# Hybrid SSD/Conformer layer: start addresses of the streamed SBUF tiles moved to 128 modulo 256 bytes, and a selection copy moved from VectorE to ScalarE

## The chip, the cores and the metric

The kernel runs on one core of a Trainium2 chip. The metric is the device time of one execution in microseconds (us). Each core has TensorE (PE, matrix products; its weight loads are listed as PEld), VectorE (DVE), ScalarE (ACT), GpSimd (POOL) and SyncE (SP, which issues the DMAs here). SBUF is the working memory, 128 partitions wide; PSUM takes the results of matmuls. A byte address below is an offset within a partition.

## The reference

One trunk layer of a diffusion backbone over 512 latent and 128 context tokens, width 1024, in float32. Cut to what matters:

```python
h = rms_norm(x, g_mix_pre) * (1 + sc1) + sh1
z, xbc, dt_raw, cf_in = split(h @ w_in)              # 1024 -> 4640 columns
xs, B, C = split(silu(dwconv1d(xbc, 3 taps)))
y = ssd_scan(xs, dt, B, C, forward) + flip(ssd_scan(flipped)) + xs * d_skip
y_ssd = rms_norm(y * silu(z))
u = silu(layer_norm(dwconv1d(cf_a * sigmoid(cf_g), 31 taps)))
x = x + g1 * rms_norm(concat([y_ssd, u]) @ w_out)
h = rms_norm(x, g_ffn_pre) * (1 + sc2) + sh2
up = dwconv(h @ w_ffn_up)                            # 1024 -> 5632, 3x3 on the latent grid
x = x + g2 * rms_norm((silu(gate) * val) @ w_ffn_down)   # 2816 -> 1024
```

The shifts, scales and gates come from `silu(c) @ w_ada`. The SSD scan works in chunks of 128 tokens and needs, for each pair of heads and each direction, the exponential of a cumulative decay.

## The kernel before, in words

All activations stand channels by tokens: a tile is 128 channels by T = 640 tokens (512 latent, then 128 context), 2560 bytes in a partition. The large products are made from two halves in the format fp32r: a weight unit of 128x1024 is fetched (`wr`), copied to a high part `wh` by ScalarE (L165), and the rest `wl` is made by GpSimd (L167). The activations are split in the same way. `mm3` (L268) then issues, for one block of 128 input channels, three products (wh with the high activation, wh with the low one, wl with the high one), and each for the columns 0 to 384 and 384 to 640: six matmuls, 384 and 256 columns in turn. The activation tile is what TensorE streams; the weights are loaded.

The stages in order of time: modulation vectors and first projections; the input projection with 36 weight units (L268, streamed tiles H0 to H15), into which the SSD of eight head pairs (`ssd`, L590 to L674) and eight 31-tap convolutions (`conv31_sum`, L721, on DVE) are woven; the output projection in two halves of the columns (streamed tiles S and H); the FFN up projection (streamed tiles T0 to T15) with its 3x3 convolution on DVE (L1090); the down projection (streamed tiles S, T and H in turn, 22 blocks for each of 8 output blocks).

Instructions are put in order by the tile framework, which places each by a simulated timeline and priorities; each engine then runs its own in that order, and waits on semaphores. The order is fixed when the program is built.

**Addresses.** The tiles of the pool `sb` are laid one after another in order of the first use of their tag, each rounded up to 32 bytes. A later tile of the same tag gets the same place. In the program before:

| tiles | start in bytes | modulo 256 |
|---|---|---|
| T0 to T15, S0 to S3 (2560 bytes each) | 17,536 to 81,280 | 128 |
| U0, U1, M3 | 64,928, 67,680, 70,432 | 160, 96, 32 |
| `asc` (64 bytes) | 83,840 | 128 |
| S4 to S17, M0 to M7 without M3, H0 to H15, HL, AT, ysq | 83,904 to 186,304 | 192 |
| `gs2` (64 bytes) | 188,864 | 192 |
| `wr`, `wh`, `wl` (4096 bytes each) | 188,928 on | 0 |

So the tile `asc` of 8 x 2 floats is what sets every tile after it 64 bytes further on.

**The selection rows.** In `decays` (inside `ssd`), `sel` picks two heads of each direction out of an identity (`ids`), each repeated 64 times: 128x256. It is copied by `ve.tensor_copy` (L608) and then loaded as the stationary operand of two matmuls of 512 columns (L612) that spread the decays; ScalarE takes the exponential (L616). `sel` has one buffer, so the copy for pair p+1 stands after the matmuls for pair p.

Of the kernel before, what the change touches and what calls it, by code (L numbers as in the profile page):

```python
# [7 lines left out]
F32 = mybir.dt.float32  # L8
F32R = mybir.dt.float32r
AF = mybir.ActivationFunctionType  # L10
# [3 lines left out]
P = 128  # L14
# [7 lines left out]
KD = D // P  # L22
# [25 lines left out]
def hybrid_layer_kernel(ctx: ExitStack, tc: tile.TileContext, xT, ct, prm, cst, wrest, wdt, idhl_d, wada1, wada2, win,  # L48
                        wout, wup, wdown, st0, yT, nsf, nsb):
    nc = tc.nc  # L50
    te, ve, ac, gp, sy = nc.tensor, nc.vector, nc.scalar, nc.gpsimd, nc.sync

    sb = ctx.enter_context(tc.tile_pool(name="sb", bufs=1))
# [6 lines left out]
    def nm(s):  # L60
        uid[0] += 1
        return f"{s}_{uid[0]}"

    def slot(tag, dt=F32, shape=(P, T)):
        return sb.tile(list(shape), dt, tag=tag, name=nm(tag))

    def psum(i):
        return ps.tile([P, 1024], F32, tag=f"P{i}", name=nm(f"ps{i}"))

    def psq(i):  # L70
        return ps.tile([P, 512], F32, tag=f"Q{i}", name=nm(f"pq{i}"))
# [32 lines left out]
    ids = sb.tile([P, 32], F32, tag="idhl", name="ids")  # L104
# [255 lines left out]
        te.matmul(pt[32 * j:32 * j + 32, 0:c1 - c0], wdts[:, k, :], xs_[k][:, c0:c1],  # L360
                  start=k < 4, stop=k >= 4, tile_position=(0, 32 * j))

    asc = sb.tile([P, KD, 2], F32, tag="asc", name="asc")
    h_hi, h_lo = [], []
    firsts = [(get_unit(unit_of[n][0]), psum((0, 2, 1)[i])) for i, n in enumerate(FIRST)]
    for s in range(1, 4):
# [184 lines left out]
    def ssd_tokens(p):  # L551

        xs = xsp[p]
        xt = xtp[p] = slot(("S14", "T13", "S14", "T13", "S14", "M2", "S14", "M2")[p])
        to_tokens(xs, xt)
        xw = []
        for d in range(2):
            o = slot(f"S{4 + d}")
            gp.tensor_tensor(hq(o), hq(xt), WD[:, :, 16 * d + 2 * p:16 * d + 2 * p + 2].unsqueeze(3)
                             .to_broadcast([P, NCH, 2, 64]), MUL)  # L560
            xw.append(o)
        xwp[p] = xw

    def ssd_states(p):
        g = p // 4
        xw = xwp[p]

        cs = []
        for d, o in enumerate((nsf, nsb)):
            pt = psq(d)  # L570
            for s in range(3):
                c = s if d == 0 else 3 - s
                te.matmul(pt[:, s * P:(s + 1) * P], btok[g][:, c * P:(c + 1) * P],  # L573
                          xw[d][:, c * P:(c + 1) * P], start=True, stop=True)
            te.matmul(pt[:, 3 * P:4 * P], xw[d][:, 4 * P:5 * P], btok[g][:, 4 * P:5 * P], start=True, stop=True)
            t = slot(f"S{12 + d}" if p % 2 else ("S16", "AT")[d])
            ac.activation(t[:, 0:4 * P], pt, AF.Copy)  # L577
            sy.dma_start(o[p], t[:, 3 * P:4 * P])
            cs.append(t)
        prev = [[stt[p][:, d, :]] for d in range(2)]  # L580
        for s in range(3):
            for d in range(2):
                tmp = sm.tile([P, P], F32, tag="adar", name=nm("stmp"), bufs=1)
                now = cs[d][:, s * P:(s + 1) * P]
                gp.tensor_tensor(tmp.rearrange("p (h q) -> p h q", h=2),
                                 prev[d][s].rearrange("p (h q) -> p h q", h=2),
                                 CDs[:, s, d, 2 * p:2 * p + 2].unsqueeze(2).to_broadcast([P, 2, 64]), MUL)
                gp.tensor_tensor(now, now, tmp, ADD)  # L588
                prev[d].append(now)
        prevs[p] = prev  # L590

    def ssd(p):
        g = p // 4
        xs, xt, prev = xsp[p], xtp[p], prevs[p]
        last = p == NPAIR - 1
        xd = []
        for d in range(2):
            o = slot(("M4", "H11")[d] if last else f"S{2 + d}")
            a = 16 * d + 2 * p
            gp.tensor_tensor(hq(o), hq(xt), DT[:, :, a:a + 2].unsqueeze(3).to_broadcast([P, NCH, 2, 64]), MUL)  # L600
            xd.append(o)

        ea = []

        def decays():
            peas = []
            sel = sm.tile([P, 2, 2, 64], F32R, tag="sel", name=nm("sel"), bufs=1)
            ve.tensor_copy(sel, ids.rearrange("p (d h) -> p d h", d=2)[:, :, 2 * p:2 * p + 2]  # L608
                           .unsqueeze(3).to_broadcast([P, 2, 2, 64]))
            for d in range(2):  # L610
                pea = psq(d)
                te.matmul(pea[:, 0:L], sel[:, d].rearrange("p h q -> p (h q)"), acHL[:, 0:L], start=True, stop=True)  # L612
                ea.append(slot(f"S{10 + d}"))
                peas.append(pea)
            for o, pea in zip(ea, peas):
                ac.activation(o[:, 0:L], pea[:, 0:L], AF.Exp)  # L616

        if last:
            decays()

        rs = {}
        for h in range(2):
            for d in range(2):
                row = 2 * p + h + 16 * d
                sel1 = idr[:, row:row + 1].to_broadcast([P, P])
                r = slot(f"{'H' if last else 'S'}{(12 if last else 6) + 2 * h + d}")
                if last:
                    pbl = psum(2 * d)
                for q, (c0, c1) in enumerate(((0, 3), (3, 5))):
                    pb = pbl[:, 512 * q:512 * q + 512] if last else psq(q)  # L630
                    te.matmul(pb[:, 0:(c1 - c0) * P], sel1, acHL[:, c0 * P:c1 * P], start=True, stop=True)  # L631
                    for c in range(c0, c1):
                        if last and d:
                            ve.tensor_scalar(r[:, c * P:(c + 1) * P], pb[:, (c - c0) * P:(c - c0 + 1) * P],
                                             ACM[:, c, row:row + 1], 0.0, SUB, MIN)
                            continue
                        ac.activation(r[:, c * P:(c + 1) * P], pb[:, (c - c0) * P:(c - c0 + 1) * P], AF.Relu,  # L637
                                      scale=-1.0, bias=ACM[:, c, row:row + 1])
                rs[h, d] = r
        if p + 1 < NPAIR:  # L640
            ssd_tokens(p + 1)
        if not last:
            decays()
        for (h, d), r in rs.items():
            ssd_exp[0] = ac.activation(r, r, AF.Exp, scale=1.0 if last and d else -1.0)  # L645
        for i, (h, d) in enumerate(rs):
            r = rs[h, d]
            (ve if i % 2 or last else gp).tensor_tensor(r, r, cbm[g][d], MUL)  # L648
        if p + 1 < NPAIR:
            ssd_states(p + 1)  # L650

        for d in range(2):
            po = psq(d)
            for c in range(4):
                te.matmul(po[:, c * P:(c + 1) * P], prev[d][c if d == 0 else 3 - c],  # L655
                          cT[g][:, c * P:(c + 1) * P], start=True, stop=True)
            ve.tensor_tensor(ea[d][:, 0:L], ea[d][:, 0:L], po[:, 0:L], MUL)
        (ve if p > 5 else gp).tensor_tensor(ea[0][:, 0:L], ea[0][:, 0:L], ea[1][:, 0:L], ADD)

        t = slot(f"T{p}")  # L660
        for q, cc in enumerate(((0, 1, 2, 3), (4,))):
            py = psq(q)
            for i, c in enumerate(cc):
                for d in range(2):
                    for h in range(2):
                        te.matmul(py[64 * h:64 * h + 64, i * P:(i + 1) * P],  # L666
                                  xd[d][:, c * P + 64 * h:c * P + 64 * h + 64],
                                  rs[h, d][:, c * P:(c + 1) * P], start=d == 0, stop=d == 1,
                                  tile_position=(0, 64 * h))
            c0, c1 = cc[0] * P, (cc[-1] + 1) * P  # L670
            ve.scalar_tensor_tensor(t[:, c0:c1], xs[:, c0:c1], prm_col("d_skip", p), py[:, 0:c1 - c0], MUL, ADD)
        yoff[p] = ea[0]
        tp[p] = t
# [105 lines left out]
    for it in seq:  # L779
        if it[0] == "proj":  # L780
# [4 lines left out]
            elif n[0] == "a":  # L785
                p = int(n[1:])
# [10 lines left out]
            elif n[:2] == "xs":  # L797
                p = int(n[2:])
# [12 lines left out]
        elif it[0] == "ssd":  # L811
            p = it[1]
# [158 lines left out]
        y_part(m, None, BOTH, out_ps[m], False, True)  # L971
        out_done(m, BOTH, out_ps[m])
    def gains():
        gg = gains_of['post'] = sb.tile([P, KD, 2], F32, tag="asc", name="gg1")
        ve.tensor_tensor(gg, modv[:, 16:24, :], prm_col("g_mix_post", 0, 8).unsqueeze(2).to_broadcast([P, 8, 2]), MUL)
        gs = gains_of['pre'] = sb.tile([P, KD, 2], F32, tag="gs2", name="gs2")
        ve.tensor_scalar(gs, modv[:, 32:40, :], 1.0, None, ADD)
        ve.tensor_tensor(gs, gs, prm_col("g_ffn_pre", 0, 8).unsqueeze(2).to_broadcast([P, 8, 2]), MUL)

    gains_of = {}  # L980
# [266 lines left out]
    with tc.issue_after(prior[0].ins):  # L1247
        for q in range(EARLY, NF):
            split_f(q)
    gg2 = sb.tile([P, KD, 2], F32, tag="asc", name="gg2")  # L1250
    ve.tensor_tensor(gg2, modv[:, 40:48, :], prm_col("g_ffn_post", 0, 8).unsqueeze(2).to_broadcast([P, 8, 2]), MUL)
    msq = sb.tile([P, T], F32, tag="ysq", name="m2sq")
    mtags = ["H5", "H6", "S8", "S9", "S16", "S17", "U0", "U1"]
# [208 lines left out]
```

## Time and profile before

| | |
|---|---|
| median of 3 runs | 1010.86 us (1010.83 to 1013.97) |
| profiled execution | 1010.71 us, of which the span of its instructions is 1008.9 us |
| mean granted TensorE clock | 0.993 |
| busy: PE, DVE, POOL, ACT | 968.3, 736.1, 588.8, 457.9 us |

Views used below: the page of the profile; busy time by stretches of time (windows); groups of instructions by line and shape; the chain of work that ended last; and the timeline, which merges neighbours of one kind into a row (start, length, kind, count). A matmul is given about 0.28 to 0.34 us in these rows, though the next one starts 0.11 to 0.18 us after it: they overlap, and what a matmul costs is read from the starts.

### The profile page before, as it was taken

How to read it: one execution, taken by the hardware profiler on the slowest of the kernel's cores; microseconds unless marked ns; L12 is line 12 of the kernel's file. 1: busy time of each engine (PE TensorE's matmuls, PEld its weight loads, DVE VectorE, ACT ScalarE, POOL GpSimd, SP SyncE). 2: the span in 40 equal slices, each digit the busy share in tenths (PEclk: the TensorE clock that was granted, in tenths of full speed). 3: DMA queues.
4: the chain of work that ended last, by engine and by line, in shares of the span. 5: the costliest groups of instructions: out<-in, count | busy, mean ns of one | idle time of the engine just before them, and what ended most of it. 6: DMA issues, size and time to landing. Idle time of an engine off the chain costs nothing.

```text
span 1008.9 us, 18834 instructions
## 1 busy us (share of the span) xinstructions
PE 968.3 (96%) x7655; PEld 933.7 (93%) x7655; DVE 736.1 (73%) x1093; ACT 457.9 (45%) x766; POOL 588.8 (58%) x426
## 2 busy tenths in 40 slices
PE   4999999999999989999989999999999999999995
PEld 2789999999999978899979999999999999999995
DVE  3789999989999998672286798998988988400004
ACT  6244556674553856842364754233233236322211
POOL 2333877888887896443473696454454456543444
PEclk9999999999999999999999999999999999999998
DMA  9622121122212111559463422222222222222212
GB/s 345 229 80 79 53 94 63 54 74 64 74 43 66 41 50 41 167 165 391 156 206 106 147 84 64 85 70 77 85 71 76 84 70 68 79 79 74 79 37 105
DMA packets 42934, 102.76 MB, mean 102 GB/s; under 512 B 4832, under 2 KB 12768, under 8 KB 42848
## 3 DMA queue, kind: packets, MB, share of 16 engines
q1 hardware_dynamic: 42848, 101.56, 30.4%
q8 instruction: 60, 0.98, 0.4%
q14 instruction: 26, 0.21, 0.1%
HBM read 97.87 MB, written 3.67 MB: 101 GB/s over the span
## 4 chain that ended last, share of the span: by engine, by line
PE 81%; DVE 7%; ACT 5%; POOL 3%; issue 2%; DMA 2%; SPq 0%; POOLq 0%; ACTq 0%; DVEq 0%
PE ps L268 67%; PE ps L1112 3%; PE pq L268 2%; POOL wl L167 2%; PE pq L313 2%; PE pq L666 1%; DVE T L760 1%; ACT wh L165 1%; DVE ps L721 1%; PE pq L655 1%; PE pq L573 1%; DMA wr<-in_wout 1%; PE pq L294 1%; PE pq L631 1%; DMA T<-in_xT 1%
## 5 line engine op out<-in xcount | busy, mean ns | idle before, releaser
L167 POOL TENSOR_TENSOR wl<-wr,wh 128x1024 fp32r<-128x1024 f32 (+3 forms) x127 | 291.7, 2297 | 293.3 <-ACT wh L165 287.4
L268 PE MATMUL ps<-H,wh 128*128 128x384 f32 (+1 forms) x1636 | 322.1, 310 | 4.9 <-DVE M L421 2.2
L165 ACT ACTIVATE wh<-wr 128x1024 fp32r<-128x1024 f32 (+3 forms) x131 | 131.7, 1006 | 342.6 <-PE ps L268 196.8
L268 PE MATMUL ps<-T,wh 128*128 128x384 f32 (+1 forms) x1472 | 273.1, 306 | 1.9 <-ACT S L1080 1.9
L268 PEld LDWEIGHTS ps<-H,wh 128*128 128x128 f32 x1636 | 249.0, 188 | 9.1 <-issue 4.5
L1090 DVE SCALAR_TENSOR_TENSOR S<-ps,prms,S 128x441 f32<-128x441 f32 (+2 forms) x336 | 233.4, 695 | 29.7 <-ACT S L1080 19.2
L268 PEld LDWEIGHTS ps<-T,wh 128*128 128x128 f32 x1472 | 219.3, 188 | 2.3 <-ACT S L1080 2.2
L721 DVE SCALAR_TENSOR_TENSOR ps<-u,prms,ps 128x655 f32<-128x655 f32 x223 | 200.7, 900 | 9.9 <-ACT ps L718 5.4
L268 PE MATMUL ps<-H,wl 128*128 128x384 f32 (+1 forms) x818 | 194.8, 310 | 0.0
L268 PE MATMUL ps<-T,wl 128*128 128x384 f32 (+1 forms) x736 | 166.7, 306 | 0.0
L268 PEld LDWEIGHTS ps<-H,wl 128*128 128x128 f32 x818 | 128.8, 188 | 1.6 <-issue 1.2
L268 PEld LDWEIGHTS ps<-T,wl 128*128 128x128 f32 x736 | 113.0, 188 | 0.0
L341 DVE RECIPROCAL rsm<-rsm 128x160 f32<-128x160 f32 (+2 forms) x9 | 7.3, 815 | 141.5 <-ACT rsm L340 141.5
L268 PE MATMUL ps<-S,wh 128*128 128x384 f32 (+1 forms) x420 | 87.5, 312 | 1.7 <-DVE M L923 1.2
L268 PEld LDWEIGHTS ps<-S,wh 128*128 128x128 f32 x420 | 65.9, 188 | 4.3 <-issue 2.5
L268 PE MATMUL ps<-S,wl 128*128 128x384 f32 (+1 forms) x210 | 54.4, 308 | 0.3 <-POOL wl L167 0.3
L637 ACT ACTIVATE S<-pq,ACM 128x128 f32<-128x128 f32 x140 | 40.9, 372 | 18.3 <-PE pq L631 18.1
L1080 ACT ACTIVATE S<-ps,prms 128x640 f32<-128x640 f32 x42 | 36.5, 868 | 0.0
L268 PEld LDWEIGHTS ps<-S,wl 128*128 128x128 f32 x210 | 35.0, 188 | 0.5 <-POOL wl L167 0.5
L588 POOL TENSOR_TENSOR S<-S,stmp 128x128 f32<-128x128 f32 x36 | 18.6, 517 | 15.1 <-ACT S L577 11.2
L1193 POOL TENSOR_TENSOR H<-S,S 128x640 f32<-128x640 f32 x16 | 25.2, 1578 | 0.0
L648 POOL TENSOR_TENSOR S<-S,M 128x640 f32<-128x640 f32 x14 | 22.1, 1577 | 4.4 <-ACT S L645 4.4
(353 smaller groups left out, 1276.7 us busy)
## 6 DMA issues: line engine op xcount, KB each, us to landing
wr<-in_wup SPq DMA_DIRECT2D x44, 512.0 KB, 3.4
wr<-in_win SPq DMA_DIRECT2D x36, 512.0 KB, 3.5
T<-in_wada SPq DMA_DIRECT2D x49, 256.0 KB, 5.4
wr<-in_wdown SPq DMA_DIRECT2D x16, 512.0 KB, 3.4
wr<-in_wout SPq DMA_DIRECT2D x13, 512.0 KB, 3.4
H<-in_wada SPq DMA_DIRECT2D x23, 256.0 KB, 5.5
S<-in_wada SPq DMA_DIRECT2D x16, 256.0 KB, 5.9
wr<-in_wdown SPq DMA_DIRECT2D x8, 384.0 KB, 3.1
```

The lines of the kernel that those rows point to most:

```text
L165: ac.activation(hi[:, :n], raw[:, :n], AF.Copy)
L167: lo_eng.tensor_tensor(lo[:, :n], raw[:, :n], hi[:, :n].bitcast(F32), SUB)
L268: last_mm[0] = te.matmul(out, w, x[:, c0:c1], start=first and i == 0, stop=last and i == 2)
L313: te.matmul(pt[32 * j:32 * j + 32, 0:P], cts[:, kc, :], w[:, j * P:(j + 1) * P], start=kc == 0, stop=kc == KD - 1, tile_position=(0, 32 * j))
L588: gp.tensor_tensor(now, now, tmp, ADD)
L637: ac.activation(r[:, c * P:(c + 1) * P], pb[:, (c - c0) * P:(c - c0 + 1) * P], AF.Relu, scale=-1.0, bias=ACM[:, c, row:row + 1])
L648: (ve if i % 2 or last else gp).tensor_tensor(r, r, cbm[g][d], MUL)
L721: ve.scalar_tensor_tensor(acc, u[:, j:j + UO], w(j), acc, MUL, ADD)
L1080: ac.activation(out, v, AF.Identity, bias=prm_col("ffn_b", i), scale=w(1, 1))
L1090: ve.scalar_tensor_tensor(ob, vl[:, r0 + a - 1:r1 + a - 1, q0 + b - 1:q1 + b - 1], w(a, b), ob, MUL, ADD)
L1112: te.matmul(pt[:, o:o + c1 - c0], w[k] if i in (1, 2) else w[:, k * P:(k + 1) * P], x[:, c0:c1], start=k == 0 and j == 0, stop=k == KD - 1 ...
L1193: gp.tensor_tensor(f_raw[q], a, b, MUL)
```

## The change

Two parts. First, `asc`, `gg1` and `gg2` (tag `asc`) become the first 16 columns of tiles that are 64 floats wide (256 bytes), and `gs2` of one that is 32 floats wide (128 bytes). All tiles of the pool that stand after `asc` move up by 192 bytes, those after `gs2` by 256. By the same rule of placing, S4 to S17, the M and H tiles, HL, AT and ysq then start at 128 modulo 256, as T0 to T15 and S0 to S3 did already; `wr`, `wh` and `wl` stay at 0. U0, U1 and M3 stay where they were. Nothing that is computed changes. Second, the copy of `sel` is an activation with Copy on ScalarE.

```diff
-    asc = sb.tile([P, KD, 2], F32, tag="asc", name="asc")
+
+    def small(tag, name, width):
+        return sb.tile([P, width], F32, tag=tag, name=name)[:, 0:2 * KD].rearrange("p (k c) -> p k c", k=KD)
+
+    asc = small("asc", "asc", 64)
...
-            ve.tensor_copy(sel, ids.rearrange("p (d h) -> p d h", d=2)[:, :, 2 * p:2 * p + 2]
-                           .unsqueeze(3).to_broadcast([P, 2, 2, 64]))
+            ac.activation(sel, ids.rearrange("p (d h) -> p d h", d=2)[:, :, 2 * p:2 * p + 2]
+                          .unsqueeze(3).to_broadcast([P, 2, 2, 64]), AF.Copy)
...
-        gg = gains_of['post'] = sb.tile([P, KD, 2], F32, tag="asc", name="gg1")
+        gg = gains_of['post'] = small("asc", "gg1", 64)
...
-        gs = gains_of['pre'] = sb.tile([P, KD, 2], F32, tag="gs2", name="gs2")
+        gs = gains_of['pre'] = small("gs2", "gs2", 32)
...
-    gg2 = sb.tile([P, KD, 2], F32, tag="asc", name="gg2")
+    gg2 = small("asc", "gg2", 64)
```

## The prediction

> **What bounds the kernel now.** I read the page first, then busy time by stretches, then the chain that ended last.
>
> ```profile
> PE 81%; DVE 7%; ACT 5%; POOL 3%; issue 2%; DMA 2%; SPq 0%; POOLq 0%; ACTq 0%; DVEq 0%
> ```
> ```profile
> core 0: us, PE busy (x) PEld busy (x) DVE busy (x) ACT busy (x) POOL busy (x), PEclk, DMA share, GB/s
> 58.00:430.00 372.00, 360.80 (x2750) 348.57 (x2749) 342.64 (x443) 218.97 (x418) 272.80 (x230) 1.00 0.22 70
> 570.00:835.00 265.00, 264.91 (x1897) 264.54 (x1898) 239.80 (x392) 97.27 (x121) 146.06 (x80) 1.00 0.25 80
> 835.00:990.00 155.00, 155.00 (x1070) 154.72 (x1070) 30.93 (x36) 47.89 (x69) 71.60 (x35) 1.00 0.22 65
> ```
>
> Four fifths of the chain is TensorE. In the up projection (570 to 835) and the down projection (835 to 990) PE never rests, at the full granted clock; there the time is the number of matmuls times the distance of their starts. In the input projection PE works 360.8 of 372 us and DVE 342.6: PE leads, and DVE is close behind. So the distance of the starts is the first thing that a new address could change. The timeline of PE shows it: each row with `wl` closes one set of six matmuls (three pairs of 384 and 256 columns), so from one `wl` row to the next is the price of a set.
>
> ```profile
> 72.61 0.47 PE L268 MATMUL ps<-H,wl 128*128 128x384 f32 x2
> ...
> 77.11 0.47 PE L268 MATMUL ps<-H,wl 128*128 128x384 f32 x2
> ```
> ```profile
> 891.62 0.45 PE L268 MATMUL ps<-H,wl 128*128 128x384 f32 x2
> ...
> 892.48 0.45 PE L268 MATMUL ps<-H,wl 128*128 128x384 f32 x2
> ```
>
> There are two rhythms: 0.90 us a set (five sets in 4.50) and 0.86, the same shapes at the same clock. The slow one costs 0.04 us more, 13.3 ns for each pair of 384 and 256 columns. H stands at 192, and has both: slow at 73 in the input projection, fast at 891 in the down projection. A whole stage shows in the mean length of a matmul of 384 columns, about 10 ns more in the slow rhythm:
>
> ```profile
> L268 PE MATMUL ps<-H,wh 128*128 128x384 f32 x620 | 197.8, 339 | 4.9 <-DVE M L421 2.2 <-ACT T L858 1.5 <-ACT u L700 1.2
> ```
> ```profile
> L268 PE MATMUL ps<-T,wh 128*128 128x384 f32 x608 | 188.0, 332 | 1.9 <-ACT S L1080 1.9
> ```
> ```profile
> L268 PE MATMUL ps<-T,wh 128*128 128x384 f32 x112 | 34.9, 341 | 0.0
> L268 PE MATMUL ps<-H,wh 128*128 128x384 f32 x92 | 28.1, 333 | 0.0
> ```
>
> These are the groups of 58 to 430 (H, mixed), 570 to 834 (T, all but eight pairs fast) and 858 to 985 (T slow, H fast). So tiles at 128 have both rhythms too, and in the down projection, where PE streams T and H in turn, the two alternate. Counted by the starts, 242 of the 867 whole pairs of the input projection are slow and 521 fast (the others are broken by a wait or change over); between 858 and 985, 174 pairs at 128 are all slow and 229 at 192 all fast.
>
> The rhythm is not a property of the address alone. It holds while PE runs on, and is drawn again when another instruction comes between. In the up projection (the timeline of PE, then the chain):
>
> ```profile
> 621.90 0.46 PE L268 MATMUL ps<-T,wl 128*128 128x384 f32 x2
> ...
> 622.80 0.46 PE L268 MATMUL ps<-T,wl 128*128 128x384 f32 x2
> 623.10 0.64 PE L268 MATMUL ps<-T,wh 128*128 128x384 f32 x3
> 623.58 0.27 PE L276 MATMUL pq<-csts,adar 128*128 128x128 f32 x1
> ```
> ```profile
> 623.85 210.27 PE ps L268 x1467
> ```
>
> The T tiles go at 0.90 us a set before one transpose of the modulation vectors, and after it at 210.27 / 1467 = 143.3 ns a matmul, 0.86 us a set, for 210 us. Where the address changes while PE runs on, as in the down projection, the rhythm turns over with it.
>
> **The change part by part.**
>
> *Copy of sel.* Eight casts leave DVE, eight copies come to ACT.
>
> ```profile
> L608 DVE CAST sel<-ids x8: 484/1648/1829, 21.6 to 395.1; 128x256 fp32r<-128x256 f32 x8
> ...
> who waited for it (us, times):
> ```
> ```profile
> 353.30 1.56 DVE sel L608
> ...
> 357.76 0.60 DVE S L657
> ...
> 358.40 1.63 PE pq L666 x25
> ```
> ```profile
> 395.05 0.40 DVE sel L608
> ```
> ```profile
> L616 ACT ACTIVATE S<-pq 128x512 f32<-128x512 f32 x16 | 8.7, 596 | 1.9 <-PE pq L612 1.8
> ```
>
> Nobody waits for `sel`. What counts is the DVE time that it takes from others. Up to about 340 PE sets the pace and a freed DVE only waits longer: nothing, and if PE had slack there it would be worth up to the rest of the casts. In the chain the cast stands twice: 1.56 us at 353, with four DVE instructions behind it and the matmuls L666 of pair 6 waiting for the last, and 0.40 us at 395. Sum: -1.96, taken as -2.0. On ACT the nearest row has twice the columns and 0.60 us, which bounds a copy from above. ACT is busy 219 of 372 us and the copy can stand anywhere in the tens of us between two uses of `sel`, so I put it at nothing; the copy has to wait for the matmuls L612 of the pair before, and behind it in ACT's queue stand the exponentials L616 and the splits of the weights, for which GpSimd and then PE wait: if two copies stand in front of these in the chain, that is 1.2 us. Bounds: -9.9 (the six casts between 130 and 375, at the median of 1.65 us, if DVE alone set this stage) to +1.2. I take -2.0, since the chain names it.
>
> *Down projection.* All streamed tiles get one address, so the rhythm should no longer turn over between tiles. All fast: 174 x 13.3 ns = -2.3 us. All slow: 229 x 13.3 = +3.05. I take fast, since the stage is entered from the up projection in the fast rhythm at 128, though single matmuls of two products are woven around 836 and 850 and can upset it.
>
> *Input projection.* 867 pairs go from 192 to 128. Both addresses have a fast and a slow rhythm of the same price, so I take the same share: 0. All fast would be -3.2 (242 pairs), all slow +6.9 (521).
>
> *Up projection.* Its tiles stand at 128 before and after, and so do the weights at 0. The rhythm is drawn at 570 and again at 620 and 624, after products of H tiles that do move. I take fast as now: 0. If slow after 624, 731 pairs x 13.3 = +9.7; if slow from 570, 897 pairs, +11.9.
>
> *Matmuls of 256 columns alone* (second half of the output projection, last half block of the down projection). Tiles at 192 go through at 0.34 us for three, tiles at 128 at 0.355:
>
> ```profile
> 994.17 0.28 PE L268 MATMUL ps<-H,wl 128*128 128x256 f32 x1
> ...
> 995.19 0.28 PE L268 MATMUL ps<-S,wl 128*128 128x256 f32 x1
> ```
> ```profile
> 562.09 0.28 PE L1112 MATMUL pq<-T,wl 128*128 128x256 f32 x1
> ...
> 563.15 0.28 PE L1112 MATMUL pq<-T,wl 128*128 128x256 f32 x1
> ```
>
> Three sets take 1.02 and 1.06 us, so 5 ns for each matmul. About 200 are concerned, half of them mixed with tiles at 128 already: +0.5 us (0 to 1.0).
>
> *The other engines on the moved tiles.* The same ACT copy takes as long from T to H as from H to T:
>
> ```profile
> L253 ACT ACTIVATE T<-H 128x640 fp32r<-128x640 f32 x8 | 5.9, 735 | 1.9 <-PE ps L268 1.4
> L253 ACT ACTIVATE H<-T 128x640 fp32r<-128x640 f32 x8 | 5.8, 738 | 10.7 <-DVE T L385 10.6
> ```
>
> 735 against 738 ns at crossed addresses: 0, and I carry that over to DVE, POOL and DMA, hidden by PE in the two FFN stages (DVE busy 239.8 of 265 us in the first).
>
> Sum against the profiled execution: 1010.7 - 2.0 - 2.3 + 0 + 0 + 0.5 = 1006.9 us, taken as 1007.0. That execution is 0.15 us under the median of the runs, and 1.8 us of it lie outside its span.
>
> [...]
>
> **The rivals.**
>
> *A, the forecast:* 1007.0; by the uncertainty of the input projection and of sel some 1002 to 1011. Chance 0.46.
>
> *B, the down projection locks in the slow rhythm.* For it: the T tiles at 128 are slow there now, after entering fast. Against: they turned where tiles of the other address came between. 1010.7 - 2.0 + 3.05 + 0.5 = 1012.3. Chance 0.22.
>
> *C, slower: the up projection locks in the slow rhythm after 624.* One mechanism: the draw after the last transpose falls the other way and nothing interrupts 731 pairs. For it: the eight slow pairs before 623.6 are on the same tiles. Against: 897 of 912 pairs are fast now. With the down projection as in A: 1006.9 + 9.7 = 1016.6. From some 290 slow pairs on it eats the 3.8 us that A gains, from some 520 on the kernel is measurably slower. Chance 0.19.
>
> *D, the address does nothing, and both rhythms stay where they are:* only sel counts, 1008.7. Chance 0.13.
>
> **How the numbers follow.** A measurement of this kernel can tell about 0.3% from no change: 3.0 us, so faster is below 1007.8 and slower above 1013.9. Of A about two thirds lie below 1007.8, of D a third, of B a tenth: 0.31 + 0.04 + 0.02, with a little for an input projection that goes all fast: 0.39. Of C nearly all is slower, and of B and A a part (an input projection that gets slower, an order of instructions that the move of sel has shifted): 0.27. The rest, 0.34, is no measurable change. Range: downwards all of the input projection fast (-3.2) and a sel gain of 5 us give 1006.9 - 3.2 - 3.0 = 1000.7; upwards C, 1016.6. The likeliest case alone has 1002 to 1011.
>
> **What would show it.** Right: between 858 and 985 the groups of T, H and S matmuls have one mean length, 331 to 333 ns; L268 on T stays at 332 between 570 and 834; the chain around 353 and 395 has no sel; L608 is an ACT row of 0.4 to 0.6 us. Wrong: a mean of 341 in the down or up projection (B, C); the same alternation as now at one address (D); a shorter stretch from 330 to 375 than sel's own 1.6 us explains (DVE bound more than I take it to). It would be wrong above all if the rhythm follows something that I do not see in these rows, since it is worth more than all else here.

## The result, and the profile after

The changed kernel is slower: 1018.93 us median (1017.07 to 1021.56) against 1010.91 for the kernel before beside it, ratio 1.0071 with the 95% interval 1.0051 to 1.0091. The profiled execution took 1019.31 us, with a span of 1017.5 us, 8.6 more than before. The forecast was 1007.0, and its range ended at 1016.6.

The page's shares of the chain and the busy time by stretches, of the changed kernel:

```profile
PE 84%; DVE 7%; ACT 3%; POOL 2%; issue 2%; DMA 1%; SPq 0%; POOLq 0%; ACTq 0%; DVEq 0%
```
```profile
core 0: us, PE busy (x) PEld busy (x) DVE busy (x) ACT busy (x) POOL busy (x), PEclk, DMA share, GB/s
58.00:430.00 372.00, 358.14 (x2716) 346.36 (x2714) 330.50 (x434) 217.39 (x420) 271.86 (x229) 0.99 0.21 66
570.00:835.00 265.00, 263.24 (x1881) 262.65 (x1880) 235.53 (x385) 101.88 (x129) 149.33 (x83) 1.00 0.26 83
835.00:990.00 155.00, 155.00 (x1076) 155.00 (x1075) 41.60 (x53) 48.64 (x69) 75.61 (x37) 1.00 0.24 72
```

VectorE has 12 us less to do between 58 and 430 (330.50 against 342.64), about what the moved copies should give, and yet TensorE got less done there (2716 instructions against 2750). The granted clock of that stretch is 0.99 in place of 1.00. That hundredth turns out to matter.

The same places of the chain that ended last, before and then after (start, length, what):

```profile
71.94 12.41 PE ps L268 x81
85.07 8.81 PE ps L268 x59
...
291.22 3.31 PE ps L268 x21
...
374.15 3.31 PE ps L268 x21
...
570.09 48.40 PE ps L268 x336
...
623.85 210.27 PE ps L268 x1467
...
874.47 114.40 PE ps L268 x771
```
```profile
73.23 13.90 PE ps L268 x81
87.85 8.81 PE ps L268 x59
...
295.12 3.43 PE ps L268 x21
...
379.46 3.44 PE ps L268 x21
...
579.06 50.63 PE ps L268 x336
...
634.93 210.27 PE ps L268 x1467
...
884.79 112.43 PE ps L268 x771
```

Read down the starts: the changed kernel is 1.3 us late at 72, 2.8 at 85, 3.9 at 291, 5.3 at 374, 9.0 at 570, 11.1 at 624, and 10.3 at 874. So it loses 9 us up to the end of the output projection, a stretch for which the forecast had a gain of 2.0 from `sel` and little else, then 2.2 us in the first 336 products of the up projection (50.63 against 48.40), nothing in the next 1467, and wins 2.0 back in the 771 of the down projection.

Two of these rows were forecast. The down projection has one rhythm now (groups of 869 to 1000, last figure before the bar is the mean in ns):

```profile
L268 PE MATMUL ps<-T,wh 128*128 128x384 f32 x112 | 33.8, 332 | 0.0
L268 PE MATMUL ps<-H,wh 128*128 128x384 f32 x98 | 29.5, 332 | 0.0
...
L268 PE MATMUL ps<-S,wh 128*128 128x384 f32 x90 | 27.1, 332 | 0.0
```

and the copy of `sel` is a row of ScalarE, 0.42 us long (L612 in the new numbering):

```profile
L612 ACT ACTIVATE sel<-ids 128x256 fp32r<-128x256 f32 x8 | 3.3, 418 | 0.0
```

One thing was in no rival. The row of 81 products at 73 us takes 1.49 us longer than before with the same work. The windows show why: first three stretches of 3.41 us, then the stretches that follow them, all of the changed kernel.

```profile
69.95:73.36 3.41, 1.16 (x9) 0.94 (x8) 3.41 (x9) 0.20 (x1) 0.00 (x0) 1.00 0.20 80
360.08:363.49 3.41, 1.22 (x22) 1.22 (x24) 3.41 (x5) 1.15 (x3) 2.89 (x6) 1.00 0.45 135
534.16:537.57 3.41, 1.49 (x15) 1.12 (x14) 3.41 (x4) 1.56 (x5) 1.98 (x1) 1.00 1.03 366
```
```profile
73.30:76.80 3.50, 3.50 (x14) 3.50 (x15) 2.90 (x6) 3.49 (x4) 0.58 (x1) 0.51 0.00 0
363.40:366.90 3.50, 3.50 (x27) 2.51 (x24) 3.50 (x5) 0.00 (x0) 2.90 (x4) 0.51 0.00 0
537.50:541.00 3.50, 3.50 (x13) 3.50 (x12) 2.59 (x6) 2.17 (x4) 1.11 (x1) 0.51 0.64 248
```

PE was busy for 1.16 to 1.49 us of 3.41 in each of the first three, and in the stretch behind each the granted clock is half (0.51). In the profiled execution of the kernel before, the granted clock is 1.00 all the time between 30 and 1002 us. An estimate from these figures (half the clock for 3.41 us): each such stretch costs up to 1.7 us where TensorE has work throughout; the row at 73 us lost 1.49.

### The profile page after: what moved, and what is told of

Same layout as the page of the kernel before. It is cut to its first block, busy times and chain, and to the rows that moved or that the text cites. A ratio compares the mean times of both kernels' runs of the same rounds, so it can differ in the third digit from the quotient of the medians.

```text
span 1017.5 us, 18830 instructions
## 1 busy us (share of the span) xinstructions
PE 973.1 (96%) x7655; PEld 939.2 (92%) x7655; DVE 722.4 (71%) x1085; ACT 460.0 (45%) x774; POOL 589.9 (58%) x426
## 4 chain that ended last, share of the span: by engine, by line
PE 84%; DVE 7%; ACT 3%; POOL 2%; issue 2%; DMA 1%; SPq 0%; POOLq 0%; ACTq 0%; DVEq 0%
PE ps L268 69%; PE ps L1116 3%; PE pq L670 2%; PE pq L268 2%; PE pq L313 2%; DVE ps L725 1%; DVE T L764 1%; PE pq L659 1%; POOL wl L167 1%; ACT wh L165 1%; PE pq L294 1%; PE pq L577 1%; DMA T<-in_xT 1%; PE pq L635 1%; PE pq L334 1%
## 5 line engine op out<-in xcount | busy, mean ns | idle before, releaser
L268 PE MATMUL ps<-H,wh 128*128 128x384 f32 (+1 forms) x1636 | 324.4, 311 | 6.2 <-DVE M L425 2.2
L268 PE MATMUL ps<-T,wh 128*128 128x384 f32 (+1 forms) x1472 | 273.3, 306 | 1.8 <-ACT S L1084 1.8
L268 PEld LDWEIGHTS ps<-H,wh 128*128 128x128 f32 x1636 | 250.9, 189 | 11.9 <-issue 5.9
L268 PEld LDWEIGHTS ps<-T,wh 128*128 128x128 f32 x1472 | 219.4, 188 | 2.1 <-ACT S L1084 2.1
L268 PE MATMUL ps<-H,wl 128*128 128x384 f32 (+1 forms) x818 | 193.8, 310 | 0.0
L268 PE MATMUL ps<-T,wl 128*128 128x384 f32 (+1 forms) x736 | 166.8, 306 | 0.0
L268 PEld LDWEIGHTS ps<-H,wl 128*128 128x128 f32 x818 | 128.9, 189 | 0.7 <-issue 0.5
L268 PEld LDWEIGHTS ps<-T,wl 128*128 128x128 f32 x736 | 112.9, 188 | 0.0
L268 PE MATMUL ps<-S,wh 128*128 128x384 f32 (+1 forms) x420 | 87.4, 311 | 1.8 <-DVE M L927 0.9
L268 PEld LDWEIGHTS ps<-S,wh 128*128 128x128 f32 x420 | 65.9, 188 | 4.0 <-issue 2.3
L268 PE MATMUL ps<-S,wl 128*128 128x384 f32 (+1 forms) x210 | 54.3, 308 | 0.3 <-POOL wl L167 0.3
L268 PEld LDWEIGHTS ps<-S,wl 128*128 128x128 f32 x210 | 35.0, 188 | 0.5 <-POOL wl L167 0.5
```

Source lines behind the costliest of these rows:

```text
L268: last_mm[0] = te.matmul(out, w, x[:, c0:c1], start=first and i == 0, stop=last and i == 2)
```

## The experiments

The shown differences left three suspects: the addresses, the moved copy, and the half-clock stretches. Ratios are against the kernel before, run beside each kernel on the same chip, with 95% intervals; medians from different chips are not compared, since the kernel before itself moved between 1010.9 and 1014.3.

**One part at a time.** Addresses only:

```diff
+    small = lambda tag, name, w: sb.tile([P, w], F32, tag=tag, name=name)[:, 0:2 * KD].rearrange("p (k c) -> p k c", k=KD)
+    asc = small("asc", "asc", 64)
...
+        gs = gains_of['pre'] = small("gs2", "gs2", 32)
```

> Only the addresses are changed (streamed tiles at 128 modulo 256, wr/wh/wl at 0); the copy of sel stays on VectorE, and with it the order of the instructions is that of before. Theory R (the address sets the rhythm of the matmul pairs, and the loss of the changed kernel is the slow rhythm drawn in the up projection's first part, +2.2, and in the output projection, +0.6, against -2.7 in the down projection): the down projection 858 to 985 all at 331 to 333 ns, -2.3 to -2.7 us against before; in all 1008 to 1011. Theory O (the 8 us are lost by the other order that the moved copy brings): 1008 to 1010, down projection as under R, stretches before 430 within 1 us of before. Theory G (the three windows of half clock at 73, 363 and 537 us make the loss, up to 1.7 us each): if the addresses bring them, the mean granted clock falls from 0.993 to 0.984 to 0.987 here, and the time is 1014 to 1018; if not, the clock stays at 0.993.

Measured: 1012.49 us, ratio 0.9995 (0.9979 to 1.0011). The moved copy only:

```diff
-            ve.tensor_copy(sel, ids.rearrange(...)...)
+            ac.activation(sel, ids.rearrange(...)..., AF.Copy)
```

> Only the copy of sel is moved to ScalarE; all addresses are those of before. Its order of instructions is that of the changed kernel. Theory R: the down projection alternates as before (T 341, H 333 ns), the sel gain of up to 2 us stands alone: 1009 to 1011. Theory O: this kernel has the whole loss before 560, +6 to +8 us there, and the down projection's 2.3 us besides: 1017 to 1020. Theory G: the clock falls to 0.984 to 0.987 only if the other order makes the idle stretches in which the gate closes; then windows of 3.4 us at half clock near 73, 363 or 537 are in its records, and each costs about 1.7 us.

Measured: 1022.08 us, ratio 1.0092 (1.0074 to 1.0111). And both parts again:

> The changed kernel again, with both parts, on the same chip as the three others. All theories: 1017 to 1020, mean granted clock 0.983 to 0.987, windows of 3.4 us at half clock between 70 and 540 us; R: up projection slow from its start to 623 again (a draw that comes out the same in each execution) ; if the rhythm is drawn at random in each execution, it comes out otherwise here and the time moves by 2 us.

Measured: 1019.03 us, ratio 1.0071 (1.0049 to 1.0093). The moved copy carries the whole loss, and the addresses none of it. In this execution of the same program the first 166 pairs of the up projection ran in the fast rhythm, where the first profile had them slow: the rhythm of that stretch is drawn in each execution (its 336 products took 50.03 us all the same, since a half-clock stretch fell into them: the granted clock from 570 to 625 us is 0.97).

The sel-only kernel also shows what the lost time looks like. The timeline of PE, before, and then sel-only, at the last L631 of pair 7 and the 40 products L666 behind it (idle time and its releaser in brackets):

```profile
396.37 0.39 PE L631 MATMUL ps<-HL,idr 128*128 128x256 f32 x1
...
397.83 2.40 PE L666 MATMUL pq<-S,S 128*64 128x128 f32 x40
```
```profile
403.35 0.39 PE L631 MATMUL ps<-HL,idr 128*128 128x256 f32 x1 [2.08 <-DVE H L634]
...
404.25 4.07 PE L666 MATMUL pq<-S,S 128*64 128x128 f32 x40
```

L631 waits 2.08 us for VectorE, where before it did not wait: behind the last L575 in front of it the old order has 13 products of L268, the new order 8. Then the clock halves (0.50 from 404.45 to 407.86 us), and the 40 products take 4.07 us in place of 2.40.

**Is it the work or the order?** The planned order changes with the moved copy. Put in order of start, by line, shape and tiles, and without the copies themselves, the profiles of before and sel-only have another instruction at 558 of TensorE's 7655 places, at 33 of VectorE's 1085 and at 62 of ScalarE's 766. With the addresses alone it is none on any engine. Two kernels have the same work on each engine (both make the copy, one result is not read) in the two orders; f1 differs from before at 4 places of TensorE's list, f2 from sel-only at 59, all before 100 us:

```diff
 f1, order of before: sel is cast on VectorE and used
+            idle = sm.tile([P, 2, 2, 64], mybir.dt.bfloat16, tag="idle", name=f"idle{p}", bufs=1)
+            ac.activation(idle, ids.rearrange(...)..., AF.Copy)
 f2, order of sel-only: sel is copied on ScalarE and used
+            ve.tensor_copy(idle, ids.rearrange(...)...)
```

> Addresses of before; sel is cast on VectorE as before and used, and ScalarE makes the same copy besides, into a tile that nobody reads. The order on VectorE, GpSimd and SP is that of before, and TensorE's but for two places; ScalarE has eight copies more. Theory O (the order makes the loss): ratio 0.999 to 1.001, clock 0.990 to 0.993. Theory A (ScalarE's copies themselves make it, since they stand in front of other ScalarE work): ratio 1.005 to 1.009, eight rows of 0.42 us and later exponentials behind them.

> Addresses of before; sel is copied on ScalarE and used, and VectorE makes the cast besides, into a tile that nobody reads. The order on TensorE, GpSimd and SP is that of sel-only but for a few places on TensorE. The same work for each engine as in the kernel with the extra ScalarE copy, in the other order. Theory O: ratio 1.007 to 1.011, as sel-only's 1.0092 or a little more, clock 0.985 to 0.987. Theory A: the same ratio as the kernel with the extra ScalarE copy, within 0.002.

Measured: f1 1015.79 us, ratio 1.0007 (0.9989 to 1.0024); f2 1022.39 us, ratio 1.0076 (1.0052 to 1.0099). Eight copies more on ScalarE cost nothing, and giving VectorE its casts back wins nothing. The order makes the loss. (One thing besides the order differs, which of the two copies the matmuls read; the profiles of f1 and f2 list nobody as waiting for it.) f2 has the idle time of sel-only in the same place, and f1 has no idle time of that size between 390 and 410 us. In f2 no half-clock stretch followed in that execution, and the 40 products took their 2.40 us:

```profile
404.83 0.38 PE L634 MATMUL ps<-HL,idr 128*128 128x256 f32 x1 [2.11 <-DVE H L637]
...
405.73 2.40 PE L669 MATMUL pq<-S,S 128*64 128x128 f32 x40
```

**Where in the order.** Four kernels move some of the eight copies: `if p == 6`, `if p != 6`, `if 0 < p < 6`, `if p == 0`.

> Addresses of before; only the copy of sel for pair 6 (the one that stood in the chain at 353 us) is on ScalarE, the seven others on VectorE. Theory O1 (the loss of sel-only, 1.0092 of before, is one place: with this copy moved, the 25 to 40 products L666 of pair 6 and the L268 products around them change places, so that PE has nothing left to fill the wait for VectorE near 396 to 401): this kernel has the new idle time of about 2 us near 397 to 401 and is 3 to 6 us slower than before (ratio 1.003 to 1.006). Theory O2 (the loss is spread over the whole order, each moved copy brings a bit): ratio within 1.002. Theory S (my forecast's sel term: 1.6 us of VectorE in the chain saved at 353): ratio 0.998 to 0.999.

Measured: ratio 1.0015 (0.9999 to 1.0031). The idle time at L631 is there (2.53 us), and the profiled execution lost 3 us between 366 and 515 us, but over its runs the kernel is hardly slower. O1 was wrong: this is one place of several.

> Addresses of before; seven copies of sel on ScalarE, that for pair 6 on VectorE. Theory O1: no new idle time near 400, ratio 1.000 to 1.004, mean clock as before (0.990 to 0.993). Theory O2: ratio 1.006 to 1.008, clock 0.986 to 0.988. If the half-clock windows come with the first stretch (the wait at 70 us) alone: clock 0.989 to 0.991, ratio 1.002 to 1.004.

Measured: 1020.36 us, ratio 1.0061 (1.0045 to 1.0078), no idle time at L631, mean clock 0.9855. O2 was nearer.

> Addresses of before; the copies of sel for pairs 1 to 5 are on ScalarE, those for 0, 6 and 7 on VectorE. The order before 130 us and after 340 us is then nearly that of before. Theory O3 (the loss of all-but-sel6, 1.0061, comes from five copies in the middle: more idle time near 265 to 295, and a half-clock window there in some executions): ratio 1.002 to 1.005, clock 0.988 to 0.990, shift at 300 us of +1 to +2. Theory O4 (the copies in the middle are hidden by TensorE, which leads there; the loss sits at the start and at the end of the stage): ratio 0.999 to 1.001, clock as before, shift at 300 us within 0.5.

Measured: 1016.55 us, ratio 1.0043 (1.0027 to 1.0059), clock 0.983 to 0.987 in its runs. TensorE's order differs from that of before at 113 places, 97 of them L268 and L631, and yet a second wait stands right behind the one that the kernel before has at 267 us (first row before, the other two this kernel):

```profile
267.27 0.91 PE L573 MATMUL pq<-S,M 128*128 128x128 f32 x6 [1.57 <-ACT S L616]
```
```profile
264.67 0.91 PE L573 MATMUL pq<-S,M 128*128 128x128 f32 x6 [1.57 <-ACT S L620]
...
266.76 1.44 PE L268 MATMUL ps<-H,wh 128*128 128x384 f32 x4 [0.95 <-DVE S L752]
```

Together they leave PE busy for 0.43 of the stretch of 3.41 us that ends at 266, and from 266 us on this execution ran 3.41 us at half clock.

> Addresses of before; only the first copy of sel (pair 0, near 20 us) is on ScalarE. What changes in the order is the start alone: the L360 and L294 products among each other before 60 us. Theory O4: the first unit's products start 0.5 to 1.3 us later (the L165 copy at 54 us in before, 55.1 to 55.3 in three executions with the order of the changed kernel), ratio 1.0005 to 1.002. Theory O3: ratio 0.999 to 1.0005.

Measured: 1014.55 us, ratio 1.0026 (1.0010 to 1.0042), more than either theory had. Its profiled execution had the first part of the up projection slow, which is 2.2 us by chance. The parts 0.0015, 0.0043 and 0.0026 add to 0.0084 of sel-only's 0.0092 (pair 7 was not tried alone, and each part has an interval of 0.0016 to either side): the loss is spread over the whole order.

**How much of it is the clock.** In every execution profiled the half-clock stretches stand on one grid of 3.413 us (in the changed kernel they start at 73.36, 363.49 and 537.57 us, 85 and 51 times 3.413 apart); its phase to the program differs from one execution to the next (1.68 us past a whole multiple of 3.413 there, 2.42 in the profile of before, where the clock changes at 29.73 and 1002.53). Between 50 and 985 us the 18 profiles hold 39 of them, and 34 follow a grid stretch in which PE was busy for 0.28 to 0.48 of the time. All 24 stretches with at most 0.40 were followed by one, and 10 of the 18 above that and below 0.50. Five more follow stretches between 0.50 and 0.64, where most stretches are not followed (0.60 and 0.63 in the profile of before were not); what decides there I can't explain. The idle time at 70 us (2.1 to 2.3 us) is in every kernel; in the profile of before the grid cut it in two, and no half-clock stretch followed either part (compare 1.16 us busy above):

```profile
67.28:70.69 3.41, 2.41 (x18) 2.16 (x16) 3.41 (x8) 0.00 (x0) 0.00 (x0) 1.00 0.43 154
70.69:74.10 3.41, 2.16 (x14) 2.19 (x15) 3.41 (x8) 2.22 (x3) 0.00 (x0) 1.00 0.00 0
```

So the number of half-clock stretches is a draw, and the order sets its odds. An estimate: with the grid laid over PE's rows of each profiled execution at all phases, and each stretch counted in which PE is busy for less than 0.48, the kernels in the old order give 1.2 to 1.8 stretches on average between 60 and 980 us, those with copies 1 to 5 moved 2.2 to 3.2. The runs agree: the mean granted clock is 0.989 to 0.991 for kernels in the old order and 0.9855 to 0.9865 for the changed kernel, sel-only, all-but-sel6, f2 and copies 1 to 5. (The estimate fails for the copy of pair 6 alone: 3.0 stretches, and yet a clock of 0.9896.) Against the kernel before on the same chip the clock is lower by 0.004 to 0.005, which is 4 to 5 us of 1012, about half of the 7 to 9 us that the full new order loses. Another 3 us are new idle time: the span less PE's busy time is 43.9 to 45.4 us in the four profiles of the new order (the changed kernel twice, sel-only, f2) and 40.6 to 42.4 in four of the old one (before, addresses-only twice, f1). What is left is as small as one draw of the rhythm, and no run assigns it. Within one program the clock shows too: addresses-only had 1009.16 us at clock 0.993 and 1015.14 at 0.987. Filling the idle time with products that nobody needs, the direct test, was not made: the added instructions would have changed the order again.

In the changed kernel's profile single idle times of TensorE of 2.25, 2.44 and 1.72 us, one ahead of each of the three half-clock stretches, were enough.

**The rhythm.** Five kernels in the order of before, with all streamed tiles at one address and the weights at another. The edits are widths alone: `cts` longer by 0 to 48 floats, `asc` 64 floats wide, `gs2` 16 to 64.

> As addresses-only, but with 64 bytes more ahead of T0: every streamed tile stands at 192 modulo 256, wr/wh/wl at 0. The order of instructions is that of before. Theory R with 'one address is what counts': the down projection is all fast (331 to 333 ns), 2.3 us less than before; the up projection's T tiles draw anew at 192. Theory R with '128 itself is the slow one': the up projection and the down projection are fast from their start, 3 to 4 us less than before, about 1007. Theories O and G: 1008 to 1010, clock 0.993, as before but for the down projection.

> Order of before, sel on VectorE; all streamed tiles at 192 modulo 256, as in all-192, but the weights wr, wh and wl at 64 in place of 0. Theory R1 (what counts is how the streamed tile stands to the weights: here 128 apart, as in addresses-only): the up projection after 624 is fast, 210 us for the 1467 matmuls, and the time is 8 to 10 us less than all-192's 1020.5, about 1011 to 1013. Theory R2 (192 itself is slow after 624): 220 us there, 1019 to 1022. Theory R3 (drawn by chance in each execution): either, and the timed runs of one program differ by up to 10 us.

> Order of before, sel on VectorE; all streamed tiles at 0 modulo 256, weights at 0. Theory R1 (distance to the weights counts: 128 is fast, 192 slow): a third value, 0, not decided by it. Theory R2 (odd multiples of 64 are the slow ones, even ones fast): fast after 624, 1011 to 1013, down projection all at 331 to 333 ns. Theory R3: either, differing from run to run.

> Order of before, sel on VectorE; streamed tiles at 128 modulo 256, weights at 64: 64 apart. Theory R1 (the distance from the weights to the streamed tile, modulo 256, sets the rhythm; 128 gave 286.7 ns a pair after 624, 192 gave 300, 0 gave 293): the same pattern as the next kernel, whichever it is, in the up projection after 624 and in the down projection. Theory R2 (the address of the streamed tile alone): fast as in addresses-only, 210 us for the 1467 matmuls, unlike the next kernel.

> Order of before, sel on VectorE; streamed tiles at 64 modulo 256, weights at 0: also 64 apart. Theory R1: in the up projection after 624 and in the down projection the same mean length of a pair as in the kernel before it (t128, w64). Theory R2: a pattern of its own, not tied to that. In time: 1009 to 1012 if fast, 1018 to 1022 if slow.

The same row of the chain, the 1467 products after the last transpose, in that order (192 and 0, 192 and 64, 0 and 0, 128 and 64, 64 and 0):

```profile
624.51 220.00 PE ps L268 x1467
```
```profile
627.57 210.27 PE ps L268 x1467
```
```profile
628.52 215.13 PE ps L268 x1467
```
```profile
627.93 215.14 PE ps L268 x1467
```
```profile
627.74 215.14 PE ps L268 x1467
```

| streamed, weights (mod 256) | apart | us for x1467 | ns a pair | ratio |
|---|---|---|---|---|
| 128, 0 (addresses-only) | 128 | 210.27 | 286.7 | 0.9995; again 0.9971 |
| 192, 64 | 128 | 210.27 | 286.7 | 0.9969; again 0.9981 |
| 192, 0 | 192 | 220.00 | 299.9 | 1.0080 (1.0062 to 1.0098) |
| 0, 0 | 0 | 215.13 | 293.3 | 1.0071 (1.0048 to 1.0095) |
| 128, 64 | 64 | 215.14 | 293.3 | 1.0082 (1.0061 to 1.0104) |
| 64, 0 | 64 | 215.14 | 293.3 | 1.0087 (1.0061 to 1.0112) |

What counts in this row is how far the streamed tile stands from the weights (R1): the two kernels 64 apart agree to 0.00 us, the two 128 apart too, and the same address 192 gives 220.00 or 210.27. At 0 and 64 apart nearly every pair takes a middle length, 291 to 298 ns, in all stages; at 128 and 192 there are the two rhythms, with draws. R2 is refuted by either address that stands twice, 192 or 128. R3, chance, does not fit: 14 profiles at 128 apart have 210.27 here, and by their times (1018.59 to 1022.27 us) all six runs of all-192 were slow. But 192 apart is not slow by itself: in the down projection all-192 is as fast as the changed kernel, whose row of 771 took 112.43 us:

```profile
884.20 112.22 PE ps L268 x771
```

Does 128 apart everywhere beat the kernel before? Both kernels were run again:

> Addresses-only again (128 and weights at 0, 128 apart), beside the next kernel on the same chip. Theory R1: 0.9995 before; the down projection gains 2.3 us, and where the up projection's first 166 pairs are drawn slow 2.2 us are lost again; ratio 0.997 to 1.000.

> Streamed tiles at 192, weights at 64 (128 apart too), again. It was 0.9969 of before. Theory R1: it differs from addresses-only by nothing but the draws of single stretches, ratio 0.996 to 0.999, within 0.002 of addresses-only. If 192/64 is better than 128/0 in itself, it is 0.002 to 0.004 below it.

Measured: addresses-only 0.9971 (0.9954 to 0.9989), 192 and 64 0.9981 (0.9965 to 0.9997). Three of the four comparisons of kernels 128 apart put them below the kernel before, by 2 to 3 us, and the fourth at no difference. The first part of the change by itself, addresses-only, is one of each: it costs nothing, and may win up to 3 us.

## Why the prediction was wrong, by its steps

*Copy of sel*, -2.0, bounds -9.9 to +1.2: this step failed. Measured alone it is +9.3 us (0.0092 of 1012.88). I priced the copy as one instruction taken out of a fixed list and one put into another, and such prices were right (0.42 us on ScalarE, 1.6 on VectorE, and f1 and f2 show that neither matters). What I left out is that the list is made anew by a simulated timeline when an instruction changes its engine. The old order had TensorE work standing in front of its waits; the new one had less. No rival had this; it stood only as half a sentence in the chance of slower. The chain, with `sel` twice in it, named a place where VectorE was late, and it could not tell what another order does there.

*The clock.* The prediction took the granted clock as given (1.00 in the rows that it showed) and the profiled 0.993 as the kernel's. It is a draw (0.986 to 0.993 in the runs of addresses-only) that depends on idle time.

*Down projection*, -2.3: right. All means are 332, and the row of 771 is 2.0 us shorter.

*Input projection*, 0: right for the rhythm. By the distances of starts between 58 and 430 us, its pairs of 290 to 310 ns cost 3.5 us above the fast length in the changed kernel, 3.6 before.

*Up projection*, 0, and rival C: its first 166 pairs were drawn slow in the profile, +2.2, and not in the second one; the 731 pairs after 624 stayed fast. C's price was right, on another address: all-192 has 220.00 against 210.27, +9.7.

*Matmuls of 256 columns alone*, +0.5: right as a sum. They start 115.7 to 117.4 ns apart before and 118.5 to 118.8 in the changed kernel, some 0.7 us for 327 of them. *Other engines on the moved tiles*, 0: addresses-only shows no loss that would speak against it. All address terms together (-2.3 + 0.5) were forecast as -1.8; addresses-only has -0.5 and -2.9 by its two ratios.

*Rival D*, the address does nothing: with other addresses the same 1467 products take 210.27, 215.14 or 220.00 us, and the T matmuls of the down projection went from a mean of 341 to 332 ns.

*"Drawn again when another instruction comes between"*: half right. At 128 and 192 apart there are draws, and all-192 has its slow and its fast stage at one distance; but the longest row goes with the distance: 128 apart was fast after 624 in every profile that has it. So it was not luck that C stayed away, though the forecast had no better ground for that than that the stage was fast before.

## What to carry to other kernels

Before pricing an edit to a program whose order is planned by a tool, build both and compare the orders; where they differ, the edit is a new schedule, and its price is not that of the instruction. To test an edit by itself, keep the order and add the work, or keep the work and change the order. In this kernel, idle time of TensorE that took six tenths or more of a 3.4 us stretch cost up to 1.67 us beyond its own length (40 products in 4.07 us in place of 2.40), and with five to six tenths a half-clock stretch followed in 10 of 18 cases, so look at the granted clock in windows of that size, and at the clocks of several runs.

## What the runs showed of the hardware

- The distance of the starts of fp32r pairs (384 and 256 columns) is 286.7, 293.3 or 299.9 ns, and goes with the distance modulo 256 bytes between the streamed tile and the weights: on average 293.3 at 0 and 64 (the 1467 products after 624 us), mostly one of the other two at 128 and 192. Why, no run shows.
- A grid stretch of 3.41 us with PE busy for at most 0.40 of it was followed by 3.41 us at half clock in 24 of 24 cases, above that and below 0.50 in 10 of 18, and from 0.50 on seldom (5 cases, up to 0.64).
- The phase of that grid to the program differs between executions (1.68 and 2.42 us past a whole multiple of 3.413 in the profiles of the changed kernel and of before), and with it, in one program, the number of half-clock stretches (0 and 3 in two profiles of addresses-only). The runs of that program spread by 6 us (1009.16 at clock 0.993 to 1015.14 at 0.987).
